# Causal attention with the keys on partitions: a first score pass for the maxima, no transposes of the probabilities, row sums on GpSimd

## The chip, the cores and the metric

The kernel runs on one core of one Trainium2 chip. The metric is the time of one execution on the device in microseconds. One core has five engines that take their instructions in order and meet through semaphores: TensorE (matmuls, PE in the profile; its weight loads are PEld), VectorE (DVE), ScalarE (ACT), GpSimd (POOL) and SyncE (SP), which only issues transfers here.

## The reference

One decoder layer over 2048 tokens of 1024 features, batch 1, in float32. Only the first sub-layer's attention changes; the rest is a convolution group beside it, a cross-attention into 256 memory tokens and an MLP of 4096 hidden features with a squared ReLU, each sub-layer between two RMS norms.

```python
def forgetting_attention(q, k, v, log_f):
    ...
    cum = jnp.cumsum(log_f, axis=1).transpose(0, 2, 1)
    ...
        logits = jnp.einsum("bqhd,bkhd->bhqk", qb, kb,
                            preferred_element_type=jnp.float32) * scale
        logits = logits + cum[:, :, q0:kl, None] - cum[:, :, None, :kl]
        ...
        mask = k_pos[None, :] <= q_pos[:, None]
        p = jax.nn.softmax(jnp.where(mask, logits, NEG_INF), axis=-1)
        outs.append(jnp.einsum("bhqk,bkhd->bqhd", p.astype(vb.dtype), vb))
```

There are 8 heads of 64 features. A softmax doesn't change with a number added to a whole row of logits, so the kernel adds only the bias of the key, not `cum` of the query.

## The kernel before

Activations are laid out with features on partitions and tokens along the free axis. The tokens go in four chunks of 512 (`TC`). Float32 products are made of float32r halves: `split` (a cast on ScalarE to the high part, a subtraction on VectorE for the low part) and `mm3`, three matmuls of high x high, high x low and low x high (L165 to L167).

The instructions are written by Python generators that are woven into one another by `drive`: a main stream (the input projections of a half, `mix_in`, then the MLP of chunks 0 to 3, `mlp`), beside it a side stream (`tail`: for each chunk the attention `attend`, then `mix_out` with the output projection, and `cross`), and the convolution's taps on VectorE as background. The numbers in `SCHED` set the ratios of the weave. The tile framework's scheduler then orders each engine's instructions by priorities and readiness, and puts in the semaphore waits. A tile of a tag takes one of the tag's slots (`BUFS`), in program order, and waits for the slot's earlier readers. `load` (L123) issues a transfer from GpSimd's queue, `store` (L126) one from SP's queue, which also brings the weights (L148).

`attend(c)` goes head by head through two blocks of 256 queries. `scores` puts queries on partitions: for each 128 queries and 512 keys two matmuls (L561, L562; the key tile holds high and low halves as 128 contraction rows, the query's high and its low part are repeated over both) into PSUM tag `sc`; VectorE adds the key bias (broadcast over the partitions by a transfer, tile `bias`) and keeps a running maximum, writing the row of logits `prow` to SBUF; the diagonal block's bias `dg` is masked by a GpSimd select (L544). When the row is whole, ScalarE makes the exponential in place and the row sum with it. `values` then turns each 128 x 128 block of `prow` with a TensorE transpose (L595) into PSUM tag `pt`, splits it into `pp`, and multiplies by the values (L611) into `o`. At the end of a head the two halves of `o` are added to `otmp`, which is stored to DRAM (`datt`); the row sums of the chunk go to DRAM (`drs`) and come back broadcast in `mix_out`.

Of the kernel before, what the change touches and what calls it, by code (L numbers as in the profile page):

```python
# [18 lines left out]
P = 128  # L19
# [3 lines left out]
TC = 512  # L23
# [27 lines left out]
# Chunk 0 takes also the slots that attention does not need then.  # L51
FIRST = dict(SIDE, rb="vk", y1="vk", q1="vk")
# [8 lines left out]
class Engine:  # L61
    """An engine; pinned, it takes its instructions in program order."""
# [18 lines left out]
class Trunk:  # L81
# [13 lines left out]
    # ---------------------------------------------------------------- tiles  # L95
# [64 lines left out]
    def mm3(self, ps, lhs, rhs, first=True, last=True):  # L160
        """ps (+)= sum over k of lhsT.T @ rhs, each operand a (high, low) pair."""
# [15 lines left out]
    def token_mean(self, ss, mean):  # L177
        """Mean over the features of ss ([128, w], partial sums): PSUM [128, w / 128], tokens on partitions."""
# [6 lines left out]
    def token_rstd(self, ss, mean):  # L185
        """1 / sqrt(mean + eps) per token, as token_mean."""
# [6 lines left out]
    def spread(self, r):  # L193
        """Values per token, [128, n] with tokens on partitions -> PSUM [128, n * 128], the same on every partition."""
# [12 lines left out]
    def pair8(self, w, name, tags):  # L207
        """Two high and two low [128, 4, w] tiles, in the order h l h l of the tags."""
# [3 lines left out]
    # ------------------------------------------------------------ constants  # L212
    def setup(self):
# [17 lines left out]
        self.carry = ct([NH, 1], "carry")  # L231
        self.rs = {c: ct([P, NH, 4], f"rs{c}") for c in range(NCH)}
# [5 lines left out]
        self.d_q = [[self.dram([2, 2, DH, TC], name="dq") for _ in range(NCH)] for _ in range(4)]  # L238
        self.d_v = [self.dram([NH, P, 8, P], name="dv") for _ in range(2)]
        self.d_nc = [self.dram([NH, HALF], name="dnc") for _ in range(2)]  # L240
# [6 lines left out]
    def setup_late(self):  # L247
# [6 lines left out]
        for t in range(4):  # L254
            self.store(self.d_u[t][:, :PAD], z)
        self.v.memset(self.wf.bitcast(F32), 0.0)
# [7 lines left out]
    # ---------------------------------------------------- memory keys/values  # L264
# [13 lines left out]
    def normed(self, xs, g, w, stag, out=None, tags=None):  # L278
        """rms_norm of xs, two [128, 4, w] tiles, in place; with tags also split, as in halves."""
# [20 lines left out]
    def halves(self, out, xs, w, tags):  # L300
        """out: the float32r (high, low) tiles of xs, two [128, 4, w] tiles."""
# [96 lines left out]
    def qk(self, h, t, ht, base):  # L398
        w = self.wtiles(self.i["w_in"][base + t], SIDE if t == 0 and base == 12 else MAIN)
        for j in range(2):  # L400
# [5 lines left out]
            for e in range(2):  # L406
                dst = (self.d_k[t][h][e, :, :, j * TC : (j + 1) * TC] if base == 12
                       else self.d_q[t][2 * h + j][e])
# [3 lines left out]
    def conv_push(self, c, t):  # L412
        """Background vector work: the depthwise convolution of channel tile t in chunk c, to DRAM."""
# [21 lines left out]
    def conv_norm(self, a, tag):  # L435
        """LayerNorm over the channels and swish of a ([128, 4, 512]), in place."""
# [22 lines left out]
    def gate(self, h, ht):  # L459
        """-cumsum(log_sigmoid(h @ w_f + b_forget)) of one half, to DRAM."""  # L460
# [29 lines left out]
        self.store(self.d_nc[h], u)  # L490

    # ------------------------------------------------------ forgetting attention
    def attend(self, c):
        """Queries of chunk c against all keys up to them, head by head."""
        nc = self.nc
        L = TC * (c + 1)
        small = L <= HALF
        pend = None
        for hd in range(NH):
            t, e = hd // 2, hd % 2  # L500
            if small:
                kv = self.tile("bk", [P, 2, L], F32R, name="kv")
# [582 lines left out]
```

## Time and profile before

| | us |
|---|---|
| median of 3 timed runs (lowest, highest) | 2849.29 (2844.85, 2852.8) |
| span of the profiled execution | 2843.6 |
| TensorE busy (share of the span) | 2779.2 (98%) |
| TensorE weight loads | 2310.6 (81%) |
| VectorE busy | 1967.2 (69%) |
| ScalarE busy | 1380.7 (49%) |
| GpSimd busy | 206.5 (7%) |

The profiled execution has no time of its own beside its span; the median of the runs is 5.7 us above it. Busy times of TensorE count pipelined matmuls, so a matmul's own duration is longer than the distance to the next one's start. The granted clock of TensorE is 0.996 of full speed in the mean.

### The profile page before, as it was taken

The numbers are of one execution on the slowest core, as the hardware profiler recorded it, in microseconds if no ns is written. First come the engines' busy times: TensorE is split into PE (matmuls) and PEld (weight loads), VectorE is DVE, ScalarE is ACT, GpSimd is POOL, SyncE is SP. The second block draws the span as 40 slices with busy tenths as digits, with TensorE's granted clock in tenths as the row PEclk, the third lists the DMA queues.
The fourth block names the chain that finished last, engine by engine and source line by source line (L and its number), as shares of the span: only waits on it lengthen the run. The fifth ranks groups of instructions, "written<-read, shape, count | busy, mean of one in ns | idle before, by whom it ended". The sixth has DMA issues, their size and how long they took to land.

```text
span 2843.6 us, 37412 instructions
## 1 busy us (share of the span) xinstructions
PE 2779.2 (98%) x14020; PEld 2310.6 (81%) x14020; DVE 1967.2 (69%) x3521; ACT 1380.7 (49%) x2164; POOL 206.5 (7%) x367
## 2 busy tenths in 40 slices
PE   7999999999999999999999999999999999999998
PEld 6889778888888887878888888788887888888887
DVE  7877896769787676788886645886665555743446
ACT  5323654345654445466554445665554445543332
POOL 0010300001110000012100001020100000000000
PEclk9999999999999999999999999999999999999999
DMA  5365744456544444455543435464524342343232
GB/s 168 117 217 170 174 128 163 141 164 200 154 137 132 124 136 145 149 151 175 138 142 119 146 108 166 129 197 129 155 94 128 126 145 93 130 144 97 96 97 81
DMA packets 141045, 398.32 MB, mean 140 GB/s; under 512 B 15248, under 2 KB 37904, under 8 KB 136000
## 3 DMA queue, kind: packets, MB, share of 16 engines
q1 hardware_dynamic: 99952, 262.40, 28.9%
q0 software_dynamic: 40912, 133.54, 16.4%
q8 instruction: 110, 1.80, 0.3%
q14 instruction: 71, 0.58, 0.1%
HBM read 330.68 MB, written 65.20 MB: 139 GB/s over the span
## 4 chain that ended last, share of the span: by engine, by line
PE 80%; issue 4%; DMA 4%; DVE 4%; ACT 2%; POOL 0%; SPq 0%; DVEq 0%; POOLq 0%; ACTq 0%
PE mm L165 18%; PE mm L166 18%; PE mm L167 18%; PE o L611 5%; PE sc L167 4%; PE sc L165 4%; PE sc L166 4%; PE pt L595 3%; PE sc L561 2%; PE sc L562 2%; DMA ks<-dk 1%; DVE acc L73 1%; DVE yacc L73 1%; DMA wr<-in_w_up_dram 1%; PE stat L182 1%
## 5 line engine op out<-in xcount | busy, mean ns | idle before, releaser
L73 ACT CAST wh<-wr 128x1024 fp32r<-128x1024 f32 x282 | 296.6, 1052 | 715.5 <-PE mm L166 634.1
L165 PE MATMUL mm<-h,wh 128*128 128x512 f32 x1504 | 597.6, 397 | 5.5 <-ACT h L73 2.6
L167 PE MATMUL mm<-h,wl 128*128 128x512 f32 x1504 | 596.9, 397 | 0.0
L166 PE MATMUL mm<-h,wh 128*128 128x512 f32 x1504 | 595.1, 396 | 1.7 <-DVE h L73 1.7
L73 DVE TENSOR_TENSOR wl<-wr,wh 128x1024 fp32r<-128x1024 f32 x282 | 345.5, 1225 | 277.2 <-ACT wh L73 276.0
L165 PE MATMUL mm<-hid,wh 128*128 128x512 f32 x992 | 395.3, 399 | 0.4 <-DVE yacc L73 0.4
L167 PE MATMUL mm<-hid,wl 128*128 128x512 f32 x992 | 392.8, 396 | 0.0
L166 PE MATMUL mm<-hid,wh 128*128 128x512 f32 x992 | 392.8, 396 | 0.0
L73 DVE SCALAR_TENSOR_TENSOR acc<-cu,convw,acc 128x512 f32<-128x512 f32 x480 | 356.9, 747 | 5.8
L165 PEld LDWEIGHTS mm<-h,wh 128*128 128x128 f32 x1504 | 283.9, 189 | 65.2 <-ACT h L73 2.9
L166 PEld LDWEIGHTS mm<-h,wh 128*128 128x128 f32 x1504 | 283.8, 189 | 60.1 <-DVE h L73 3.2
L167 PEld LDWEIGHTS mm<-h,wl 128*128 128x128 f32 x1504 | 283.6, 189 | 58.4
L73 DVE TENSOR_TENSOR yacc<-mm,yacc 128x512 f32<-128x512 f32 (+1 forms) x232 | 155.0, 669 | 160.3 <-PE mm L167 158.7
L73 DVE TENSOR_TENSOR pp<-pt,pp 128x512 fp32r<-128x512 f32 (+1 forms) x288 | 186.9, 656 | 68.0 <-ACT pp L73 66.6
L73 ACT CAST pp<-pt 128x512 fp32r<-128x512 f32 (+1 forms) x288 | 159.5, 560 | 124.6 <-PE pt L595 116.0
L165 PEld LDWEIGHTS mm<-hid,wh 128*128 128x128 f32 x992 | 186.3, 188 | 39.6 <-DVE yacc L73 1.5
L167 PEld LDWEIGHTS mm<-hid,wl 128*128 128x128 f32 x992 | 186.5, 188 | 38.5 <-issue 0.5
L166 PEld LDWEIGHTS mm<-hid,wh 128*128 128x128 f32 x992 | 186.6, 188 | 36.5 <-DVE hid L73 0.3
L595 PE MATMUL pt<-ident,prow 128*128 128x128 f32 x1088 | 199.3, 274 | 1.0 <-ACT prow L73 0.9
L73 ACT ACTIVATE prow<-prow,mx 128x128 f32<-128x128 f32 (+15 forms) x128 | 154.2, 1205 | 76.7 <-DVE mx L73 74.1
L73 DVE CUSTOM_DVE_ANT_0 prow<-sc,bias 128x512 f32<-128x512 f32 (+3 forms) x288 | 166.8, 596 | 34.3 <-PE sc L562 29.6
L611 PE MATMUL o<-pp,vv 128*128 128x256 f32 (+1 forms) x832 | 178.8, 299 | 8.6 <-DVE pp L73 7.9
(234 smaller groups left out, 4585.5 us busy)
## 6 DMA issues: line engine op xcount, KB each, us to landing
wr<-in_w_up_dram SPq DMA_DIRECT2D x128, 512.0 KB, 3.5
wr<-in_w_down_dram SPq DMA_DIRECT2D x128, 512.0 KB, 3.5
wr<-in_w_in_dram SPq DMA_DIRECT2D x32, 512.0 KB, 4.4
q<-dq POOLq DMA_DIRECT2D x64, 256.0 KB, 6.1
wr<-in_w_out_dram SPq DMA_DIRECT2D x32, 512.0 KB, 3.5
dx<-y SPq DMA_DIRECT2D x16, 1024.0 KB, 4.2
bias<-dnc POOLq DMA_DIRECT2D x32, 512.0 KB, 5.7
x<-in_x_dram POOLq DMA_DIRECT2D x12, 1024.0 KB, 5.9
```

Source lines behind the costliest of these rows:

```text
L73: ins = op(*args, **kw)
L165: mm(ps, ah, bh, start=first and j == 0, stop=False)
L166: mm(ps, ah, bl, start=False, stop=False)
L167: mm(ps, al, bh, start=False, stop=last and j == n - 1)
L182: self.nc.tensor.matmul(ps[:, t : t + 1], ss[:, t * P : (t + 1) * P], mean, start=True, stop=True)
L561: nc.tensor.matmul(ps[:, :w], q[:, 0, qs], ks[:, k0 : k0 + w], start=True, stop=False)
L562: nc.tensor.matmul(ps[:, :w], q[:, 1, qs], ks[:, k0 : k0 + w], start=False, stop=True)
L595: nc.tensor.transpose(pt[:, at : at + P], prow[t][:, (k0 + k) * P : (k0 + k + 1) * P], self.ident)
L611: nc.tensor.matmul(out, v[:, g + k], rhs, start=g == 0 and n == 0, stop=g == nk - 2 and n == 3)
```

## The change

Attention is done in two passes over a head, both generators; `peaks` runs some tiles ahead of `values` (n + 4 steps at the start of a chunk, n = 4(c + 1) key tiles, then one step of each in turn).

- `peaks` puts queries on partitions as before but computes one product only: the query's high part against the keys' high part, with two more contraction rows that hold the key bias's high and low part against ones (66 rows; L565). VectorE takes the maximum straight from PSUM; the diagonal block gets a mask first. The four negated maxima of a head, one column for each 128 queries, are transposed on TensorE (L587), copied to `mr`, stored to DRAM (`dm`) by SP's queue, and loaded by GpSimd's queue as one row of the query tile `q`.
- `values` puts keys on partitions: two matmuls (L608 with 128 rows, L609 with 67: the low query part, the bias rows and the row of negated maxima) give the shifted logits of 128 keys against up to 512 queries in PSUM tag `pt`. ScalarE makes the exponential from PSUM to the SBUF tile `p`; on the four diagonal tiles GpSimd zeroes the masked part (L614). `p` is split to `pp` and goes into the value product (L626) without a transpose. GpSimd adds `p` into an accumulator, the first tile's `p` (L621). At the end of the head four products with ones (L633) make the row sums.
- The gate also splits its bias and stores both parts (`d_kx`, in the place of `d_nc`); rows of ones are written to DRAM at the start. Tags: `vk` goes, `bq` and `ba` come, `vs` has 3 slots for 4; the y and rb tiles of chunk 0 are made of narrower ones.

```diff
-    "mk": 6, "bk": 7, "vk": 1,                            # 8 KB
+    "mk": 6, "bk": 7,
...
-    "ms": 4, "bs": 3, "vs": 4,                         # 2 KB
+    "ms": 4, "bs": 3, "bq": 2, "ba": 2, "vs": 3,
...
+        one = self.tile("mu", [NH, 2 * TC], name="one")
...
+        for t in range(4):
+            for c in range(NCH):
+                self.load(self.d_q[t][c][:, :, DH:].rearrange("e l o t -> (e l) o t"),
+                          one[:4].rearrange("p (o t) -> p o t", o=2))
...
-        self.store(self.d_nc[h], u)
+        self.split(e.bitcast(F32R), z.bitcast(F32R), u)
+        self.store(self.d_kx[h][:, 0], e)
+        self.store(self.d_kx[h][:, 1], z)
...
+        n = 4 * (c + 1)
...
+        p1, p2 = chain(peaks), chain(sums)
+        for _ in range(n + 4):
+            cost = next(p1, None)
+            if cost is not None:
+                yield cost
+        for cost in p2:
+            yield cost
+            cost = next(p1, None)
+            if cost is not None:
+                yield cost
...
+    def peaks(self, c, hd, T):
...
+        T["kb"] = kb = self.tile("bk", [P, L], F32R, name="kb")
+        for g, w, sl in self.halves_of(L):
+            self.load(kb[:DH, sl], self.d_k[t][g][e, 0, :, :w])
+            self.load(kb[DH : DH + 3, sl], self.d_kx[g][hd, :, :w])
+        q1 = self.tile("bq", [P, TC], F32R, name="q1")
+        self.load(q1[: DH + 2], self.d_q[t][c][e, 0])
+        mx = self.st([P, 4, 4], name="mx")
+        for t4 in range(4):
+            Lt = c * TC + (t4 + 1) * P
+            for n, k0 in enumerate(range(0, Lt, TC)):
...
+                nc.tensor.matmul(ps[:, :w], q1[: DH + 2, t4 * P : (t4 + 1) * P], kb[: DH + 2, k0 : k0 + w],
+                                 start=True, stop=True)
+                if k0 + w == Lt:
...
+                else:
+                    self.v.tensor_reduce(mx[:, t4, n : n + 1], ps, axis=AX.X, op=ALU.max)
+                yield 0.23 * w / TC
...
+        self.v.tensor_reduce(nm, mx[:, :, : c + 1], axis=AX.X, op=ALU.max, negate=True)
+        ps = self.ps("stat")
+        nc.tensor.transpose(ps[:4, :P], nm, self.ident)
+        mr = self.tile("row", [4, P], F32R, name="mr")
+        self.a.copy(mr, ps[:4, :P])
+        self.store(self.d_m[c][hd], mr.bitcast(F32))
+        self.load(T["q"][DH + 2 : DH + 3, 1], self.d_m[c][hd].rearrange("a b -> (a b)")[None])
...
-                        nc.tensor.transpose(
-                            pt[:, at : at + P], prow[t][:, (k0 + k) * P : (k0 + k + 1) * P], self.ident)
...
-                self.split(pp[:, 0, :at], pp[:, 1, :at], pt[:, :at])
...
+                nc.tensor.matmul(ps[:, q0:], ka[:, js], q[:, 0, q0:], start=True, stop=False)
+                nc.tensor.matmul(ps[:, q0:], kb[: DH + 3, js], q[: DH + 3, 1, q0:], start=False, stop=True)
+                p = self.tile("ba" if j == 0 else "bs", [P, TC], name="p")
+                self.a.activation(p[:, q0:], ps[:, q0:], AF.Exp)
+                if j >= 4 * c:
+                    dg = p[:, q0 : q0 + P]
+                    nc.gpsimd.affine_select(out=dg, in_=dg, pattern=[[1, P]], compare_op=ALU.is_ge, fill=0.0,
+                                            base=0, channel_multiplier=-1)
...
+                self.split(pp[:, 0, q0:], pp[:, 1, q0:], p[:, q0:])
+                if j == 0:
+                    acc = p
+                else:
+                    nc.gpsimd.tensor_tensor(out=acc[:, q0:], in0=acc[:, q0:], in1=p[:, q0:], op=ALU.add)
...
+                for l in range(2):
+                    nc.tensor.matmul(o[:, z:], v[:, k], pp[:, l, z:], start=k == 0 and l == 0,
+                                     stop=k == nk - 1 and l == 1)
...
+        for t in range(4):
+            nc.tensor.matmul(ps[:, t : t + 1], acc[:, t * P : (t + 1) * P], self.ones, start=True, stop=True)
+        self.a.copy(self.rs[c][:, hd], ps[:, :4])
```

Two places show how the order moves. On TensorE, in the attention of chunk 3, late in the chunk, the rows of before are these (`o<-pp,vv` is a value product, `pt<-ident,prow` a transpose, `sc<-ks,q` a score product, `mm<-h,wl` the main stream's):

```order
L595 MATMUL pt_17824<-ident,prow_17563 128x128
L167 MATMUL mm_17772<-h_2691_15806,wl_17769 128x512
L595 MATMUL pt_17824<-ident,prow_17564 128x128
L595 MATMUL pt_17824<-ident,prow_17563 128x128
L595 MATMUL pt_17824<-ident,prow_17564 128x128
L611 MATMUL o_17756<-pp_17817,vv_17330 128x256 [waits Activation_49]
L611 MATMUL o_17756<-pp_17817,vv_17330 128x256 [waits DVE_49]
L611 MATMUL o_17756<-pp_17817,vv_17330 128x256 x2
L561 MATMUL sc_17836<-ks_17729,q_17738 128x512
L562 MATMUL sc_17836<-ks_17729,q_17738 128x512
```

And in the order of the changed kernel, in head 6 of chunk 3 (`pt<-q,ka` and `pt<-q,kb` are the two score products of a key tile, `o<-pp,vv` the value products, `mm<-hid,wh` the main stream's):

```order
L609 MATMUL pt_17379<-q_16982,kb_16787 128x512
L608 MATMUL pt_17403<-q_16982,ka_16980 128x512 [waits Activation_49]
L626 MATMUL o_17279<-pp_17310,vv_16981 128x512 [waits Activation_49]
L609 MATMUL pt_17403<-q_16982,kb_16787 128x512
L165 MATMUL mm_17995<-hid_17316,wh_17977 128x512
L626 MATMUL o_17279<-pp_17310,vv_16981 128x512 [waits DVE_49]
L626 MATMUL o_17279<-pp_17370,vv_16981 128x512 [waits Activation_49]
L608 MATMUL pt_17417<-q_16982,ka_16980 128x512 [waits Activation_49]
L626 MATMUL o_17279<-pp_17370,vv_16981 128x512 [waits DVE_49]
L609 MATMUL pt_17417<-q_16982,kb_16787 128x512
L608 MATMUL pt_17431<-q_16982,ka_16980 128x512 [waits Activation_49]
L626 MATMUL o_17279<-pp_17384,vv_16981 128x512 [waits Activation_49]
```

The transposes are gone and scores and value products have 512 columns; a value product stands two to three key tiles behind its scores, each with a wait for ScalarE's cast or VectorE's subtraction, and in this part one row of twelve is the main stream's.

On GpSimd, around the end of a head of chunk 2, the rows of before are transfer issues (L123) with a select of the diagonal bias now and then:

```order
L123 DMA vv_12478<-dv_127 128x1024 [waits DMASW2_49,PE_49,Activation_49]
L123 DMA bias_12479<-dnc_130 128x512
L123 DMA vv_12478<-dv_128 128x512 [waits DMASW4_49]
L123 DMA bias_12814<-dnc_129 128x1024 [waits DMASW5_49,DVE_49,Pool_49]
L544 AFFINE_SELECT dg_12489<-bias_12479 128x256 [waits DMAHW4_49,DMASW3_49]
L123 DMA bias_12814<-dnc_130 128x512 [waits DMASW6_49]
L123 DMA q_12821<-dq_125 64x2x512 [waits DMASW7_49]
L123 DMA q_12821<-dq_125 64x2x512 [waits DMASW0_49]
```

In the changed kernel, around the end of head 2 of chunk 3 (p_15285 is that head's accumulator; `q<-dm` is the row of maxima of the head that comes next, and its wait on DMAHW0 is for the store by SP's queue; the `kb` tile belongs to the head after that):

```order
L614 AFFINE_SELECT p_15602<-p_15602 128x128 [waits DVE_49,Activation_49]
L621 TENSOR_TENSOR p_15285<-p_15285,p_15602 128x384 [waits Pool_49]
L123 DMA vv_15384<-dv_166 128x1024 [waits DMASW0_49,PE_49]
L123 DMA vv_15384<-dv_167 128x1024 [waits DMASW1_49]
L123 DMA q_15385<-dm_159 1x16x32 [waits DMAHW0_49,DMASW2_49]
L123 DMA kb_15588<-dk_110 64x1024 [waits DMASW3_49,PE_49]
L123 DMA kb_15588<-dkx_132 3x1024 [waits DMASW4_49]
L123 DMA kb_15588<-dk_111 64x1024 [waits DMASW5_49]
L123 DMA kb_15588<-dkx_133 3x1024 [waits DMASW6_49]
L614 AFFINE_SELECT p_15617<-p_15617 128x128 [waits DVE_49,Activation_49]
L614 AFFINE_SELECT p_15632<-p_15632 128x128 [waits Activation_49]
```

Selects and adds of the diagonal tiles now stand between the issues, and the last two selects of the head stand behind the load of the next head's maxima.

## Rows read from the trace of the kernel before

**Rows 1.** The page's first part: span, busy time, share and instructions by engine.

```profile
span 2843.6 us, 37412 instructions
...
PE 2779.2 (98%) x14020; PEld 2310.6 (81%) x14020; DVE 1967.2 (69%) x3521; ACT 1380.7 (49%) x2164; POOL 206.5 (7%) x367
```

**Rows 2.** Attention of chunks 0, 2, 3, all: us, then busy by engine, clock, DMA, GB/s.

```profile
282.00:372.00 90.00, 84.52 (x474) 68.21 (x474) 78.60 (x244) 55.99 (x127) 28.96 (x54) 1.00 0.70 179
...
1164.00:1440.00 276.00, 269.72 (x1460) 224.46 (x1459) 241.98 (x532) 158.68 (x248) 44.66 (x78) 0.98 0.52 155
1766.00:2096.00 330.00, 322.00 (x1811) 270.09 (x1810) 240.73 (x554) 192.84 (x289) 42.38 (x78) 1.00 0.50 149
sum 896.00, PE 872.53 PEld 732.51 DVE 726.59 ACT 525.50 POOL 147.71; mean PE 218.13 PEld 183.13 DVE 181.65 ACT 131.38 POOL 36.93
```

**Rows 3.** TensorE's timeline in three places: start, duration, line, operation, tiles, shape.

```profile
1901.09 0.39 PE L165 MATMUL mm<-h,wh 128*128 128x512 f32 x1
...
1902.22 0.39 PE L165 MATMUL mm<-h,wh 128*128 128x512 f32 x1
...
1904.18 0.60 PE L595 MATMUL pt<-ident,prow 128*128 128x128 f32 x4
1904.53 0.48 PE L165 MATMUL mm<-h,wh 128*128 128x512 f32 x1
...
2007.98 0.28 PE L611 MATMUL o<-pp,vv 128*128 128x256 f32 x1
2008.11 0.39 PE L166 MATMUL mm<-h,wh 128*128 128x512 f32 x1
```

**Rows 4.** Groups of TensorE's instructions by shape: count, busy us, mean ns, idle before.

```profile
L595 PE MATMUL pt<-ident,prow 128*128 128x128 f32 x1088 | 199.3, 274 | 1.0 <-ACT prow L73 0.9 <-DVE pp L73 0.2
L611 PE MATMUL o<-pp,vv 128*128 128x256 f32 x768 | 171.9, 303 | 8.2 <-DVE pp L73 7.4 <-ACT pp L73 0.6
...
L611 PE MATMUL o<-pp,kv 128*128 128x256 f32 x256 | 58.6, 301 | 1.8 <-DVE pp L73 0.6 <-ACT pp L73 0.5 <-DVE otmp L73 0.2
```

**Rows 5.** Groups by shape on VectorE and ScalarE: count, busy us, mean ns, idle before.

```profile
L73 DVE TENSOR_TENSOR pp<-pt,pp 128x512 fp32r<-128x512 f32 x224 | 152.4, 686 | 63.5 <-ACT pp L73 62.2
...
L73 DVE TENSOR_REDUCE mmx<-sc 128x2 f32<-128x512 f32 x32 | 21.9, 684 | 11.0 <-PE sc L167 10.9
...
L73 ACT CAST pp<-pt 128x512 fp32r<-128x512 f32 x224 | 130.1, 584 | 108.4 <-PE pt L595 100.0 <-DVE mx L73 3.1 <-DVE wl L73 2.6
```

**Rows 6.** Groups on GpSimd, then durations (min/median/max) of the selects of L544.

```profile
L544 POOL TENSOR_SCALAR_AFFINE_SELECT dg<-bias 128x256 f32<-128x256 f32 x64 | 36.0, 565 | 177.4 <-DMA datt<-otmp 77.9 <-DMA bias<-dnc 45.0 <-DVE mx L73 38.9
...
L123 POOL DMA_DIRECT2D bias<-dnc x48 | 26.6, 556 | 182.5 <-issue 88.0 <-PE sc L562 40.8 <-ACT h L73 22.8
...
masks.py:199 POOL TENSOR_SCALAR_AFFINE_SELECT ident<-ident 128x128 f32<-128x128 f32 x1 | 0.3, 318 | 0.1
...
L544 POOL TENSOR_SCALAR_AFFINE_SELECT dg<-bias x64: 398/426/1387, 282.4 to 2088.0; 128x256 f32<-128x256 f32 x64
```

**Rows 7.** Timeline of a select on GpSimd, a subtraction beside it, and the subtraction's group.

```profile
1878.56 0.45 POOL L544 TENSOR_SCALAR_AFFINE_SELECT dg<-bias 128x256 f32<-128x256 f32 x1
...
1878.59 0.97 DVE L73 TENSOR_TENSOR hid<-relu,hid 128x512 fp32r<-128x512 f32 x1
...
L73 DVE TENSOR_TENSOR hid<-relu,hid 128x512 fp32r<-128x512 f32 x128 | 88.4, 690 | 34.1 <-ACT hid L73 34.0
```

**Rows 8.** A copy's group; transfers (KB, us to landing); SP's waits (total, times, longest).

```profile
L73 ACT COPY rt<-stat 32x128 f32<-32x128 f32 x4 | 1.0, 256 | 0.8 <-PE stat L535 0.7
...
q<-dq POOLq DMA_DIRECT2D x64, 256.0 KB, 6.1
...
cu<-du POOLq DMA_DIRECT2D x16, 271.0 KB, 3.8
...
drs<-rt SPq DMA_DIRECT2D x4, 16.0 KB, 1.9
...
SPq L148 <- DVE wl L73: 1373.1, 262, 18.5
```

More of the change, by code (lines that the diff above doesn't have):

```diff
@@ L255, in setup_late @@
             self.store(self.d_u[t][:, :PAD], z)
+        one = self.tile("mu", [NH, 2 * TC], name="one")
+        self.v.memset(one, 1.0)
+        for h in range(2):
+            self.load(self.d_kx[h][:, 2], one[:, :HALF])
+        for t in range(4):
+            for c in range(NCH):
+                self.load(self.d_q[t][c][:, :, DH:].rearrange("e l o t -> (e l) o t"),
+                          one[:4].rearrange("p (o t) -> p o t", o=2))
         self.v.memset(self.wf.bitcast(F32), 0.0)
@@ L531, in attend, with chain @@
-        yield from self.values(*pend)
+            T = {}
+            peaks.append(self.peaks(c, hd, T))
+            sums.append(self.values(c, hd, T))
+        n = 4 * (c + 1)
+        def chain(gens):
+            for g in gens:
+                yield from g
+        p1, p2 = chain(peaks), chain(sums)
[8 more added lines that the diff above has]
+                yield cost
@@ L538, in attend, with halves_of @@
         self.store(self.d_rs[c].rearrange("a (b c) -> (a b) c", c=P), rt)
-    def scores(self, c, hd, b, ks, bias, q, small, rows):
-        nc = self.nc
-        L = c * TC + (b + 1) * QB
-        dg = self.tile("bs", [P, 2, P], name="dg")
-        nc.gpsimd.affine_select(
-            out=dg, in_=bias[:, L - QB : L].rearrange("p (t k) -> p t k", k=P), pattern=[[0, 2], [-1, P]],
-            compare_op=ALU.is_ge, fill=NEG, base=0, channel_multiplier=1)
-        if small:
-            pr = self.tile("bk", [P, 2, HALF], name="prow")
-            rows += [pr[:, 0, :L], pr[:, 1, :L]]
-        else:
-            rows += [self.tile("bk", [P, L], name="prow") for _ in range(2)]
-        mx = self.st([P, 2, 8], name="mx")
-        for t in range(2):
-            Lt = L - (1 - t) * P
-            p = rows[t][:, :Lt]
-            qs = slice(b * QB + t * P, b * QB + (t + 1) * P)
-            n = 0
-            for k0 in range(0, Lt, TC):
+    def halves_of(self, L):
+        for g in range((L + HALF - 1) // HALF):
+            w = min(HALF, L - g * HALF)
+            yield g, w, slice(g * HALF, g * HALF + w)
@@ L579, in scores @@
-                yield 0.43 * w / TC
-    def values(self, c, hd, b, prow, v):
+                        out=ps[:, :w], in0=ps[:, :w], in1=self.mask[:, TC - w :], op0=ALU.add, op1=ALU.max,
+                        scale=1.0, scalar=-3e38, accum_out=mx[:, t4, n : n + 1])
+                else:
+                    self.v.tensor_reduce(mx[:, t4, n : n + 1], ps, axis=AX.X, op=ALU.max)
+                yield 0.23 * w / TC
+            if t4 == 1:
+                T["ka"] = ka = self.tile("bk", [P, L], F32R, name="ka")
+                T["v"] = v = self.tile("bk", [P, L // P, P], F32R, name="vv")
+                T["q"] = q = self.tile("bu", [P, 2, TC], F32R, name="q")
+                for g, w, sl in self.halves_of(L):
+                    self.load(ka[:, sl], self.d_k[t][g][e, :, :, :w].rearrange("l d t -> (l d) t"))
+                    self.load(v[:, 8 * g : 8 * g + w // P], self.d_v[g][hd, :, : w // P])
+                for r in range(2):
+                    self.load(q[r * DH : (r + 1) * DH, 0], self.d_q[t][c][e, 0, :DH])
+                self.load(q[: DH + 2, 1], self.d_q[t][c][e, 1])
@@ L633, in residual, with pairs @@
         for k in range(KT):
-            y = ys[k // 4][:, k % 4]
+            y = ys[k // 2][:, k % 2]
             self.mul(y, y, r)
             self.add(y, y, xs[k // 4][:, k % 4])
-            if k % 4 == 3:
-                self.store(dst[:, k - 3 : k + 1], ys[k // 4])
+            if k % 2:
+                self.store(dst[:, k - 1 : k + 1], ys[k // 2])
             yield SCHED["y1"]
+    def pairs(self, g, role, name):
+        if role in g and role != "k":
+            return [self.tile(g[role], [P, 2, TC], name=name) for _ in range(2)]
+        y = self.tile(g["k"], [P, 4, TC], name=name)
+        return [y[:, 0:2], y[:, 2:4]]
     def mix_out(self, c, g):
@@ L655, in mix_out @@
             if b == 1:
-                self.mul(at, at, rb)
+                for k in range(2):
+                    self.mul(at[:, 2 * k : 2 * k + 2], at[:, 2 * k : 2 * k + 2], rb[k])
             self.split(hl[0][b], hl[1][b], (cu, at)[b])
@@ L684, in cross @@
         kt = self.ktiles(h2)
-        q2 = [self.tile(t, [P, 2, 2, TC], F32R, name="mq") for t in (g["k"], g.get("q1", g["k"]))]
+        q2 = []
         for f in range(MH):
+            if f == 2 and "q1" in g:
+                q2 += [[self.tile(t, [P, TC], F32R, name="mq") for t in g["q1"]] for _ in range(2)]
+            elif f % 2 == 0:
+                mq = self.tile(g["k"], [P, 2, 2, TC], F32R, name="mq")
+                q2 += [[mq[:, h, 0], mq[:, h, 1]] for h in range(2)]
             w = self.wtiles(i["w_mq"][f], g)
```

134 lines of the change are left out of this document (44 added, 90 removed).

## Prediction

> **What bounds the kernel now.** I read the page's busy times first: in a span of 2843.6 us TensorE is busy 2779.2 us, VectorE 1967.2, ScalarE 1380.7 and GpSimd 206.5 [rows 1]. So the kernel ends when TensorE has gone through its rows, and a change is worth the TensorE rows that it takes out, less the waits that it puts between them. The averages hide the stretches in which attention runs, so I then took a table by stretch, one stretch for the attention of each chunk [rows 2]. TensorE is busy 84.5 of 90 us in that of chunk 0, 269.7 of 276 in that of chunk 2, 322.0 of 330 in that of chunk 3 and 872.5 of 896 over the four: 23.5 us idle in all. VectorE is close behind: 87% of chunk 0's stretch and 88% of chunk 2's. GpSimd has most of its time free. Thus there are 23.5 us of waits to win in attention, and VectorE is the engine with the least room for being held up.
>
> A matmul's own duration overlaps the next one's, so rows are priced by the distance between starts [rows 3]: five matmuls of 512 columns take 1.13 us (0.227 each), one of 256 columns 0.13 (I use 0.12, nearer to half of 0.227), four transposes 0.35 (0.0875 each).
>
> **The change part by part.**
>
> TensorE, removed: 1088 transposes [rows 4] at 0.0875, 95 us. The two score passes keep their columns (2 x 512 per key tile and 512 queries in the place of 2 x 512 per 128 queries and 512 keys). The value products go from 1024 of 256 columns [rows 4] and 128 of 128 to fewer and wider ones, by the order 448 of 512 columns and 64 each of 384, 256 and 128, at prices by columns (0.227, 0.17, 0.12, 0.06) 124 us in the place of 131: 7 us less. Added: the peaks pass, 224 matmuls of 512 columns and 32 each of 384, 256 and 128, 51 + 11 = 62 us; 128 products of one column with ones for the row sums, no dearer than a transpose, 11 us; 32 small transposes, 3 us. Shorter moving operands can't go below these prices by much: the 128-column rows are 2 us in all. Sum: -95 - 7 + 62 + 11 + 3 = **-26 us**.
>
> TensorE's waits: the 23.5 us of the four stretches [rows 2] belong to chains that the change replaces (bias load, running maximum, exponential over a whole row). I take all of them out, **-24 us**, and put in the new ones below. At worst none goes.
>
> The chain of a key tile: the second pass does score, exponential, cast, subtraction, value product. Per full key tile of 512 queries TensorE has two score, two value and about one peaks matmul, 5 x 0.227 = 1.14 us. ScalarE has a cast (584 ns) and an exponential from PSUM (nearest row: the same cast, since it too reads 512 columns of PSUM): 1.17. VectorE has a subtraction (686) and a maximum over 512 columns (684): 1.37 [rows 5]. So where nothing of the main stream stands between, a tile costs 0.23 us more than its matmuls. The order shows where that is: heads 2 to 6 of chunk 0 and heads 5 to 7 of chunks 2 and 3, where the side stream runs with one main row to every three to eight of attention (first two fences of the order); that is 5 x 4 + 3 x 12 + 3 x 16 = 104 key tiles, 104 x 0.23 = **+24 us**. Elsewhere main matmuls, about as many as attention's, cover the difference; without that cover the other 216 tiles would cost 50 us more.
>
> GpSimd's adds: 288 of them replace sums that ScalarE gave with its exponential. No row of before is an add on GpSimd. The nearest is the select: 318 ns for 128 columns, 398 at the least and 565 in the mean for 256 [rows 6]. Continued at 80 ns per 128 columns that is 0.56 us for 512; twice the mean gives 1.13. The add reads two operands, so I take 1.13. A head of chunk 3 then has 13.5 full adds, 4 selects and 13 DMA issues of 0.56 [rows 6], 15.3 + 1.3 + 7.3 = 24 us, against 18 us of attention matmuls when dense and 40 of the stretch when not (330 / 8): alone it does not bound. The page "GPSIMD Engine Reference" of the Trainium skill, section 3.1, says that the Vector engine should keep elementwise work, an add taking GpSimd 1.96 times as long; on the 690 ns of a VectorE row here that would be an estimate of 1.35 us, which no run here shows yet.
>
> But adds also hold VectorE up. In before a subtraction of the MLP, both its operands in SBUF, started at 1878.59, 0.03 us behind a select of 0.45 us, and took 0.97 us, where its kind takes 0.69 in the mean [rows 7]: 0.28 us longer. The change makes all 320 subtractions of the value pass such (their source was PSUM), and puts an add beside each. At 0.28 us for each dense tile that is 104 x 0.28 = **+29 us**; at nothing, 0; at the full length of an add, 104 x 1.13 = 118 us. I take the row's figure, since the add, like the select, is over before many subtractions begin. "SBUF - State Buffer" in the Trainium skill, section "SBUF: two separate sides", speaks against the change here: a VectorE operation with two SBUF inputs and a GpSimd operation share a port pair under an exclusive lock, and the later waits out the earlier's whole length. The row agrees with that as far as a select of 0.45 us can tell; by the rule a longer add holds longer, toward the 118.
>
> The maximum's way back: for each head the four maxima go through a transpose (0.09), a copy (nearest row 256 ns), a store by SP (a 16 KB store lands in 1.9 us), a GpSimd load issue (0.56) and the landing, 3.8 us for the quickest of POOL's loads here and 6.1 for q [rows 8]: 6.6 to 8.9 us; with SP's 1.9 for the landing too, 4.7. The first L609 of the head needs it. Counted in the order from L587 to that row at the distances of [rows 3] there are 2.3 us in heads 3 to 6 of chunk 0, and 5.0 to 7.4 in most others. What is lacking over all heads sums to 10 us at 4.7, 32 at 6.6 and 89 at 8.9. SP's store also stands behind weight loads that wait 5.2 us each in the mean (1373.1 / 262), and GpSimd's load of the maxima, in waiting for that store, holds the selects of the head before that are queued behind it (last fence of the order). I take **+40 us**, a little over the middle value.
>
> Costed at nothing: the ones rows written to DRAM at the start (18 issues, 10 us of an otherwise idle GpSimd under the first projections; 10 us if they stood on the path); the gate's split and second store, under the half's projections; the narrower tiles of chunk 0.
>
> Sum: -26 - 24 + 24 + 29 + 40 = **+43 us**. The profiled execution's span of 2843.6 becomes 2887; the median of the runs, 2849.3, lies 5.7 above that span, so 2892 in the runs' terms.
>
> **The rivals.**
>
> *Faster:* the reordering hides it all. For: the program is a weave of streams and the order has two or more matmuls of the MLP or the projections beside most attention rows; before's own chain cost only 23.5 us of idle time. Against: the dense heads, and VectorE at 87 to 88%. If neither the 24 nor the 29 us appear and the way back costs 10: 2849 - 50 + 10 = 2809; if the waits of before stay too, 2833. Point 2821.
>
> *No change:* adds at 0.56 us that rarely meet a subtraction, so no 29, and the way back at the middle value: 2849 - 50 + 24 + 32 = 2855, down to 2845 with the way back at 22.
>
> *GpSimd becomes the bound:* an add that in its turn waits for VectorE's operations, and lies in front of the selects on which the diagonal's value products wait, and ahead of the row sums on TensorE (L633 waits for GpSimd's last add of a head, and TensorE takes its rows in order). With an add at 2.26 us, twice the price taken, a dense head of chunk 3 has 30.5 + 1.3 + 7.3 = 39 us of GpSimd for 18 of TensorE, of chunk 2 (9.5 adds) 30 for 14, of chunk 0 (1.5 adds, 9 issues) 10 for 4: 3 x 21 + 3 x 16 + 5 x 6 = 141 us in the place of the 24 + 29. That gives 2849 - 50 + 141 + 40 = 2980. It decides from some 1.5 us per add, waits included. For: the held-up subtraction [rows 7]. Against: GpSimd was at 13 to 32% of the stretches [rows 2].
>
> **How the numbers follow.** My forecast, some waits in the dense heads and at the maxima (2860 to 2930): 0.42. GpSimd as the bound (2930 to 3010): 0.23. No change (2840 to 2860): 0.12. Faster, 2800 to 2840: 0.23. The likeliest is the first, 2892. A measurement of this kernel can tell 0.3%, 8.5 us, from no change; of the no-change case two thirds lie within it and the rest falls to both sides: faster 0.25, same 0.08, slower 0.67. The range leaves out about a tenth at each end: 2817 to 2985. Within the likeliest case alone it is 2860 to 2930.
>
> **What would show it.** TensorE rows: no 128 x 128 transposes of prow, 224 one-matmul peaks, and the sum of distances 26 us down. Dense heads: in chunk 2 and 3 VectorE busy over 90% in heads 5 to 7, TensorE waiting before L626 for the subtraction; subtractions beside adds longer than 0.69 us, and adds over 1.1. Way back: TensorE idle before L609 on the DMA of dm, above all in heads 3 to 6 of chunk 0. GpSimd as bound would show as waits before L633, L614's readers and the p buffers' exponentials. I am wrong if adds come out near 0.56 us and subtractions stay at 0.69, or if the idle time before L609 is gone: then the time is below 2850.

## The result, and the profile after

The changed kernel takes 3064.61 us in the median (3061.45 to 3066.62, 4 runs); the kernel before took 2847.07 beside it. The ratio is 1.0766 (95% interval 1.075 to 1.0783): 217 us slower, where 43 were forecast.

The page of the changed kernel begins so, with the granted clock by slices (answers to [rows 1]); the last line is that of the kernel before:

```profile
span 3064.8 us, 35914 instructions
...
PE 2890.9 (94%) x13028; PEld 2315.0 (76%) x13028; DVE 2125.9 (69%) x3048; ACT 1395.2 (46%) x2293; POOL 680.4 (22%) x891
...
PEclk9999699998799999998899999999999999999999
...
PEclk9999999999999999999999999999999999999999
```

TensorE has fewer instructions than before and is yet busy 112 us longer, and idle 174 us (3064.8 - 2890.9) in the place of 64. Its granted clock was 9 tenths or more in each slice of before; now slices fall to 6, 7 and 8. The four attention stretches, from the first score row to the last value row of a chunk (answers to [rows 2]; the columns are those):

```profile
237.00:389.00 152.00, 140.89 (x765) 118.35 (x766) 111.51 (x207) 62.30 (x128) 63.55 (x120) 0.83 0.50 138
667.00:893.00 226.00, 196.71 (x972) 161.57 (x970) 181.83 (x288) 108.57 (x218) 116.24 (x154) 0.86 0.47 133
1251.00:1558.00 307.00, 266.30 (x1087) 197.92 (x1086) 268.75 (x386) 164.00 (x302) 188.62 (x215) 0.93 0.40 114
1886.00:2265.00 379.00, 335.81 (x1369) 247.03 (x1368) 304.58 (x412) 207.80 (x379) 225.07 (x243) 0.95 0.37 108
```

By the same marks they were 129, 191, 268 and 337 us before and are 152, 226, 307 and 379 now, 139 us more; and from the end of the last one the program takes 800 us to its end (706 before), since less of the main stream got done beside attention. GpSimd is busy in 42 to 61% of each (13 to 32% in [rows 2]), and the clock is 0.83 to 0.95. TensorE's longest waits: line, releaser, us in total, times, longest:

```profile
PE o L626 <- DVE pp L73: 67.4, 89, 3.0
PE stat L633 <- POOL p L621: 13.7, 13, 2.9
...
PE o L626 <- ACT pp L73: 10.9, 12, 3.2
...
PE pt L609 <- DMA q<-dm: 6.0, 4, 2.2
PE pt L608 <- ACT p L73: 5.2, 8, 1.4
```

The groups that answer to [rows 5] and [rows 6], and the products with ones:

```profile
L73 DVE TENSOR_TENSOR pp<-p,pp 128x512 fp32r<-128x512 f32 x224 | 249.1, 1129 | 45.6 <-ACT pp L73 44.7
...
L73 DVE TENSOR_REDUCE mx<-sc 128x1 f32<-128x512 f32 x192 | 129.4, 682 | 21.9 <-PE sc L565 21.2
...
L621 POOL TENSOR_TENSOR p<-p,p 128x512 f32<-128x512 f32 x192 | 291.2, 1517 | 107.3 <-ACT p L73 56.4 <-DVE pp L73 38.9 <-DVE mx L73 2.9
...
L614 POOL TENSOR_SCALAR_AFFINE_SELECT p<-p 128x128 f32<-128x128 f32 x128 | 60.7, 480 | 56.1 <-ACT p L73 52.3 <-DVE otmp L73 2.2 <-DVE pp L73 1.1
...
L633 PE MATMUL stat<-ones,p 128*128 128x1 f32 x256 | 45.5, 257 | 19.1 <-POOL p L621 13.7 <-ACT mr L73 4.2 <-DMA vv<-dv 0.5
```

A full subtraction takes 1129 ns, not 686. A full add takes 1517 ns in the mean. The maximum's way back (L609 waiting for q<-dm) is 6 us of TensorE's time. And L633 stands there 256 times, though the program issues 128: each float32 product is two rows.

What happens between an add and a subtraction is plain in the timeline. Two places, GpSimd first, then VectorE (start, duration):

```profile
2060.29 1.28 POOL L621 TENSOR_TENSOR p<-p,p 128x512 f32<-128x512 f32 x1 [3.62 <-ACT p L73]
...
2060.83 1.29 DVE L73 TENSOR_TENSOR pp<-p,pp 128x512 fp32r<-128x512 f32 x1 [1.33 <-ACT pp L73]
...
2205.04 1.27 POOL L621 TENSOR_TENSOR p<-p,p 128x512 f32<-128x512 f32 x1 [5.19 <-ACT p L73]
...
2205.98 0.88 DVE L73 TENSOR_TENSOR pp<-p,pp 128x512 fp32r<-128x512 f32 x1 [1.12 <-ACT pp L73]
```

The add of 2060.29 ends at 2061.57, and the subtraction that started 0.54 us into it ends at 2062.12, 0.55 later. The add of 2205.04 ends at 2206.31, and the subtraction that started 0.94 into it ends at 2206.86, again 0.55 later. Of the full adds that took under 1.30 us, 31 had a full subtraction start inside them; each of the 31 ended 0.55 or 0.56 us behind the add, wherever in the add it had started. So the subtraction waits until the add is over; it does not share a rate with it. Over all 224 full subtractions, the 61 that meet no add take 0.687 us in the mean, the 130 that start inside one 1.360, and the other 33, in which an add starts, 1.03.

TensorE's own rate in such a stretch, late in chunk 0 (two windows one behind the other, then rows of the second one's timeline):

```profile
300.00:324.00 24.00, 22.38 (x113) 17.27 (x111) 16.16 (x36) 10.09 (x27) 17.78 (x34) 1.00 0.52 139
324.00:376.00 52.00, 44.82 (x135) 32.86 (x136) 34.61 (x70) 20.92 (x53) 37.34 (x71) 0.52 0.41 106
...
340.29 0.58 PE L626 MATMUL o<-pp,vv 128*128 128x256 f32 x1 [0.52 <-DVE pp L73]
...
341.92 0.63 PE L609 MATMUL pt<-q,kb 67*128 67x512 f32 x1
342.35 0.63 PE L565 MATMUL sc<-kb,q 66*128 66x512 f32 x1
342.77 0.52 PE L609 MATMUL pt<-q,kb 67*128 67x384 f32 x1
...
346.25 0.59 PE L633 MATMUL stat<-ones,p 128*128 128x1 f32 x2 [0.73 <-ACT mr L73]
```

From 341.92 to 342.35 and to 342.77, matmuls of 512 columns stand 0.42 to 0.43 us apart, where [rows 3] had 0.227. In the first window the clock is 1.00 and TensorE busy in 22.4 of 24 us; in the second it is 0.52, the lower of its two levels (1.2 GHz of 2.4) nearly throughout, and that is the stretch in which it waits for subtractions and sums again and again (the idle times in brackets). Over the whole span the clock records have 227 us at the lower level, where there were 25 before.

### The profile page after: what moved, and what is told of

Same layout as the page of the kernel before. It is cut to its first block, busy times and chain, and to the rows that moved or that the text cites. A ratio compares the mean times of both kernels' runs of the same rounds, so it can differ in the third digit from the quotient of the medians.

```text
span 3064.8 us, 35914 instructions
## 1 busy us (share of the span) xinstructions
PE 2890.9 (94%) x13028; PEld 2315.0 (76%) x13028; DVE 2125.9 (69%) x3048; ACT 1395.2 (46%) x2293; POOL 680.4 (22%) x891
## 4 chain that ended last, share of the span: by engine, by line
PE 74%; DVE 12%; DMA 4%; POOL 4%; ACT 3%; issue 3%; POOLq 0%; ACTq 0%; DVEq 0%; SPq 0%
PE mm L166 18%; PE mm L165 18%; PE mm L167 17%; DVE pp L73 4%; PE sc L167 4%; PE sc L165 4%; PE sc L166 4%; POOL p L621 3%; PE o L626 2%; PE sc L565 1%; DVE acc L73 1%; DVE yacc L73 1%; DVE mx L73 1%; PE pt L609 1%; PE pt L608 1%
## 5 line engine op out<-in xcount | busy, mean ns | idle before, releaser
L621 POOL TENSOR_TENSOR p<-p,p 128x512 f32<-128x512 f32 (+3 forms) x288 | 370.8, 1288 | 111.3 <-ACT p L73 56.4
L73 DVE SCALAR_TENSOR_TENSOR acc<-cu,convw,acc 128x512 f32<-128x512 f32 x480 | 378.3, 788 | 7.2
L73 DVE TENSOR_TENSOR pp<-p,pp 128x512 fp32r<-128x512 f32 (+1 forms) x320 | 305.4, 969 | 84.3 <-ACT pp L73 83.1
L626 PE MATMUL o<-pp,vv 128*128 128x512 f32 (+3 forms) x640 | 244.9, 433 | 79.6 <-DVE pp L73 67.4
L626 PEld LDWEIGHTS o<-pp,vv 128*128 128x128 f32 x640 | 130.5, 215 | 161.6 <-DVE pp L73 121.9
L73 ACT CAST pp<-p 128x512 fp32r<-128x512 f32 (+1 forms) x320 | 174.8, 555 | 134.7 <-PE o L626 74.9
L73 ACT ACTIVATE p<-pt 128x512 f32<-128x512 f32 (+2 forms) x320 | 163.9, 531 | 150.7 <-PE pt L609 81.5
```

Of the source, the lines that this page charges most:

```text
L73: ins = op(*args, **kw)
L621: nc.gpsimd.tensor_tensor(out=acc[:, q0:], in0=acc[:, q0:], in1=p[:, q0:], op=ALU.add)
L626: nc.tensor.matmul(o[:, z:], v[:, k], pp[:, l, z:], start=k == 0 and l == 0, stop=k == nk - 1 and l == 1)
```

## The experiments

In all of them the scheduler orders anew, so an edit moves other rows too; only the two with the gap have the same order of TensorE's rows, row for row, as their parent. All ratios are to the kernel before, on the same chip in the same session. Between sessions the median of that kernel moved from 2844.9 to 2850.6 us, so a difference of times from two sessions is uncertain by some us. In the two runs without adds the row sums are those of a constant, so they are read for their time only.

| run | median us | ratio, 95% interval |
|---|---|---|
| changed kernel | 3064.6 | 1.0766 (1.075 to 1.0783) |
| no adds | 2927.5 | 1.0286 (1.0269 to 1.0303) |
| adds on VectorE | 2996.6 | 1.0528 (1.051 to 1.0546) |
| subtraction from PSUM | 3014.3 | 1.0593 (1.0577 to 1.0608) |
| no way back | 3047.7 | 1.0714 (1.0694 to 1.0734) |
| 128-byte gap in the kernel before | 2864.9 | 1.0062 (1.0042 to 1.0083) |
| the same gap in the changed kernel | 3045.9 | 1.0697 (1.0668 to 1.0727) |
| no first pass, adds on GpSimd | 3002.1 | 1.0549 (1.0526 to 1.0571) |
| no first pass, adds on VectorE | 2875.7 | 1.0099 (1.0076 to 1.0122) |
| ... and slots | 2815.8 | 0.9885 (0.9866 to 0.9904) |
| ... and more cover | 2770.5 | 0.9725 (0.9703 to 0.9747) |
| no adds, gap, more cover | 2873.6 | 1.0089 (1.0069 to 1.011) |
| gap, more cover | 2973.3 | 1.0445 (1.042 to 1.047) |

Theory A: an add on GpSimd holds up the subtraction, TensorE waits, and its clock falls after the waits. Theory B, the rival: the two passes are too dense and the maxima come late, whatever GpSimd does. Theory C: GpSimd is late because it is occupied, and the port pair of the prediction has no part in it.

**Without adds.**

```diff
-                else:
-                    nc.gpsimd.tensor_tensor(out=acc[:, q0:], in0=acc[:, q0:], in1=p[:, q0:], op=ALU.add)
```

> The 288 adds on GpSimd are left out; the products for the row sums read a constant, so the sums are those of ones. Theory A (an add holds the port that a subtraction of two SBUF operands needs, TensorE waits for the subtraction, and its clock falls after such waits): the 512-column subtractions go from 1129 ns back to 690, TensorE's wait for them from 67 us to under 20, granted clock from 0.963 to over 0.985, time 2840 to 2890. Theory B (the two-pass chain itself is too dense and the maxima come late, whatever GpSimd does): over 2980.

2927.5 us, so the adds cost 137 us of the 217. Subtractions are back at the length of [rows 5], and TensorE's wait for them fell from 67.4 us to 3.2:

```profile
span 2927.6 us, 35375 instructions
...
PE 2828.6 (97%) x13028; PEld 2289.7 (78%) x13028; DVE 1966.3 (67%) x3048; ACT 1388.0 (47%) x2293; POOL 307.9 (11%) x604
...
L73 DVE TENSOR_TENSOR pp<-p,pp 128x512 fp32r<-128x512 f32 x224 | 151.7, 687 | 62.5 <-ACT pp L73 61.4
...
PE o L626 <- DVE pp L73: 3.2, 7, 1.0
```

But 83 us stay over the kernel before, more than theory A allowed, and the granted clock came back to 0.979 only, not over 0.985: the adds are the larger part, not all. This run takes away the adds' collisions and their load on GpSimd together, so it speaks against theory B alone; A and C both fit it. Transfers queued behind the adds are not what it won: TensorE waits for the row of maxima (q<-dm) 6.3 us here and 6.0 in the changed kernel.

**Adds on VectorE.** `nc.gpsimd` becomes `self.v` in that line.

> The same 288 adds go to VectorE. Theory A: no collision is left, but VectorE gets 288 more operations, 240 full ones at 0.69 us, 165 us; subtractions at 0.69, time 2880 to 2960. Theory B: VectorE is the engine of the dense chain, so the time is no better than 3060. Theory C (GpSimd's occupancy, not the port, makes it late: row sums and selects stand behind adds): as A, but then the next run stays slow.

2996.6 us: 68 better than on GpSimd, although VectorE has 288 more operations now. It is above theory A's upper end, 2960, and under theory B's 3060; subtractions take 688 ns. It is 69 worse than without adds: the price of the adds as VectorE's work.

**The subtraction's source in PSUM.**

```diff
-                p = self.tile("ba" if j == 0 else "bs", [P, TC], name="p")
+                full = 0 < j < 4 * c
+                p = ps if full else self.tile("ba" if j == 0 else "bs", [P, TC], name="p")
...
-                    nc.gpsimd.tensor_tensor(out=acc[:, q0:], in0=acc[:, q0:], in1=p[:, q0:], op=ALU.add)
+                    nc.gpsimd.tensor_tensor(out=acc[:, q0:], in0=acc[:, q0:], in1=pp[:, 0].bitcast(F32) if full else p[:, q0:], op=ALU.add)
```

> All adds stay on GpSimd. For the key tiles off the diagonal and behind the first, the exponential is written back into PSUM, so the subtraction reads one operand from PSUM and one from SBUF; the add takes the high part of p, so the row sums leave out the low parts of those tiles. Theory A: subtractions of these tiles at 0.69 us beside adds of 1.27, time under 2930. Theory C: adds take as much of GpSimd as before, time over 3000.

Both kinds of subtraction stand side by side in this run, then its adds:

```profile
L73 DVE TENSOR_TENSOR pp<-pt,pp 128x512 fp32r<-128x512 f32 x168 | 114.8, 685 | 39.7 <-ACT pp L73 37.8
...
L73 DVE TENSOR_TENSOR pp<-p,pp 128x512 fp32r<-128x512 f32 x56 | 52.9, 945 | 21.6 <-ACT pp L73 20.6
...
L622 POOL TENSOR_TENSOR p<-p,pp 128x512 f32<-128x512 f32 x168 | 228.9, 1363 | 137.1 <-ACT pp L73 81.6 <-DVE pp L73 39.9 <-ACT wh L73 7.5
```

With one operand in PSUM the subtraction takes 685 ns beside adds of 1363; with both in SBUF 945. So the collision is one of SBUF operands, as theory A says of the mechanism. TensorE's wait for subtractions fell from 67.4 us to 21.0. But the time only fell by 50 us, to 3014, where theory A gave under 2930 and theory C over 3000. So theory C may hold for a part. GpSimd's selects on the diagonal tiles stand behind adds, and ScalarE's casts wait for the selects; in the changed kernel, in this run, and without adds:

```profile
ACT pp L73 <- POOL p L614: 44.1, 45, 6.4
...
ACT pp L73 <- POOL p L615: 54.6, 65, 2.3
...
ACT pp L73 <- POOL p L616: 18.4, 36, 2.7
```

Row sums that wait for the last add (L634, 18.2 us), adds that now wait for the cast, and the first and diagonal tiles, still in SBUF, may keep the rest. No run takes these apart: some 50 of the 137 us went with most of the collisions, and how the others divide between the collision and GpSimd's load stays open.

**No way back for the maxima.** The first pass runs, its result goes unused, and the row of q that held the maxima is the query's own gate bias, negated, stored once by the gate and loaded with q.

```diff
-        self.load(T["q"][DH + 2 : DH + 3, 1], self.d_m[c][hd].rearrange("a b -> (a b)")[None])
...
+                self.load(q[DH + 2 : DH + 3, 1],
+                          self.d_kx[c // 2][hd, 3:4, c % 2 * TC : (c % 2 + 1) * TC])
```

> The first pass runs in full, but its maxima are not used: each query's logits are shifted by its own gate bias instead (a row written once by the gate and loaded with q), so no head waits for the way back through DRAM. Theory A: 10 to 30 us better than the changed kernel, 3035 to 3055. Theory B: the way back and what GpSimd holds up in waiting for it are the larger part, under 2980.

3047.7 us, 17 better, inside theory A's 10 to 30. The way back is a small term.

**A gap of 128 bytes.** Every row of the main stream `mm<-h,wh` in the changed kernel was a little longer from start to start, even at the end of the program, where no attention runs: 0.2333 us ((2967.96 - 2961.66) / 27), against 0.227 in [rows 3].

```profile
2961.66 0.40 PE L165 MATMUL mm<-h,wh 128*128 128x512 f32 x1
...
2967.96 0.39 PE L165 MATMUL mm<-h,wh 128*128 128x512 f32 x1
```

The tile `vs` has slots of 2176 bytes per partition; with 3 of them instead of 4 everything behind moves, and the distance from the activations `h` to the weights, as the two programs lay out their tiles, changes from a multiple of 512 bytes (74240) to 92544, which is 384 over one. The edit is one unused tile behind the first `vs` tile:

```diff
+        gap = self.tile("gap", [P, 32], name="gap")
+        self.v.memset(gap, 0.0)
```

> The kernel before, with 128 unused bytes per partition between the main stream's activation tiles and all tiles behind them, so that the distance from its activations to its weights is no longer a multiple of 512 bytes, as in the changed kernel. Theory D (that distance slows the main stream's 512-column matmuls from 0.227 to 0.232 us from start to start): the rows mm<-h at 0.231 to 0.233, 4512 of them at 0.005 more, 20 to 28 us slower, 2865 to 2875. Against it (the distances are longer because of what the other engines read and write): 2840 to 2852.

> The changed kernel with the same 128 bytes, which here bring the distance back to a multiple of 512. Theory D: mm<-h back at 0.227, 15 to 28 us faster than the changed kernel, 3035 to 3050. Against it: 3058 to 3070.

In the kernel before it costs 0.62% (0.42 to 0.83), some 18 us, a little under theory D's 20 to 28; in the changed kernel it saves 19 (3064.6 to 3045.9). Both bear out theory D. In the profile of the former, activations that moved with the weights (hid) and those that did not (h) follow one another:

```profile
2713.02 0.39 PE L167 MATMUL mm<-hid,wl 128*128 128x512 f32 x1
...
2720.50 0.39 PE L167 MATMUL mm<-hid,wl 128*128 128x512 f32 x1
2720.72 0.40 PE L165 MATMUL mm<-h,wh 128*128 128x512 f32 x1
...
2722.35 0.39 PE L166 MATMUL mm<-h,wh 128*128 128x512 f32 x1
```

hid: 33 steps in 7.48 us, 0.2267. h: 7 steps in 1.63 us, 0.233. So 19 us of the change are due to where a tile landed. This holds for the main stream's rows: the score rows sc<-ks,q of the kernel before, whose tiles lie a multiple of 512 bytes apart too, stand 0.231 apart in the median, with the gap and without it, so the distance is not the whole rule.

**No first pass.** With the gate bias as the shift the exponent of a query and an earlier key is their scaled product plus a sum of log gates. That sum is never above zero, so softmax needs no maximum as long as the scaled products alone stay small, and `peaks` is left with its loads, issued one head ahead. The gap is in.

> No first pass: the logits of a query are shifted by its own gate bias (as in the run without the way back), the loads of a head are issued one head ahead, and the 128 bytes are in. GpSimd still adds. Takes out 62 us of peaks rows on TensorE and 150 to 215 us of maxima on VectorE. Theory A: the adds go on holding up the subtractions, so most of their 137 us stay: 2900 to 2980. Theory B (the first pass and VectorE's load make the chain too dense): under 2850.

> As the run before, with the adds on VectorE, which has had the maxima taken off it. Theory A: no add stands beside a subtraction, VectorE's load is under that of the kernel before, TensorE's rows 90 us shorter than the kernel before's: 2760 to 2840, faster than both kernels. Theory B: the same, since the first pass is gone; if the chain of score, exponential, cast, subtraction, product is itself too long for the order, it stays over 2850.

With the adds on GpSimd 3002.1 us, above what either theory gave, on VectorE 2875.7. The same 288 adds are 126 us dearer on GpSimd, now that VectorE has time. That alone fits theory C too; the waits of the run with the adds on GpSimd speak for A as the larger part (argued from waits, not taken apart), since TensorE waits four times as long for subtractions as for the sums that need the last add, and subtractions take 1200 ns:

```profile
L73 DVE TENSOR_TENSOR pp<-p,pp 128x512 fp32r<-128x512 f32 x224 | 264.0, 1200 | 123.5 <-ACT pp L73 122.7
...
PE o L596 <- DVE pp L73: 73.6, 95, 2.8
...
PE stat L603 <- POOL p L591: 18.1, 22, 3.7
```

But 2875.7 missed the 2840 that A allowed; over 2850 was forecast for a chain that is itself too long. The waits with the adds on VectorE show where it waits (ScalarE, then TensorE):

```profile
ACT p L73 <- DMA datt<-otmp: 52.0, 17, 6.0
...
PE pt L578 <- ACT p L73: 30.4, 18, 4.8
PE o L596 <- ACT pp L73: 29.1, 15, 5.0
```

An exponential of a head's fourth to sixth key tile waits 3 us each, 17 times, until the last head's otmp has landed in DRAM, because p and otmp share three slots.

**Slots, then cover.**

```diff
-    "ms": 4, "bs": 3, "bq": 2, "ba": 2, "vs": 3,
+    "ms": 4, "bs": 4, "bq": 2, "ba": 2, "vs": 3,
...
-                ps = self.ps("pt")
+                ps = self.ps("sc" if j % 2 else "pt")
...
-        tmp = self.tile("bs", [P, TC], name="otmp")
+        tmp = self.tile("bq", [P, TC], name="otmp")
```

> The run without the first pass and with adds on VectorE, and three slot changes: a head's otmp has slots of its own (it held one of the three slots of p until its store had landed; ScalarE waited 52 us for that), p has 4 slots, the scores alternate between the PSUM tags pt and sc. If slots make its waits (30 us before L578, 29 before L596): 2810 to 2850, equal to or better than the kernel before. If the chain itself is too dense where the side stream runs alone: no better than 2865.

2815.8 us, 60 better, and under the kernel before; the three slot changes were not tried one by one. Then the declared cost, by which the weave deals out the main stream:

```diff
-                yield 0.9 * (TC - q0) / TC
+                yield 1.2 * (TC - q0) / TC
```

> As the run before, with the declared cost of a key tile raised from 0.9 to 1.2, so that the weave puts more of the main stream beside each tile and attention takes longer. If density is what is left: 2790 to 2840, better than the run before by 10 to 40 us. If not, the same within 10 us, or worse where the side stream no longer fits beside the main one.

2770.5 us, another 45 better and 2.75% (2.53 to 2.97) under the kernel before. Its page and longest waits:

```profile
span 2773.4 us, 34353 instructions
...
PE 2698.5 (97%) x12676; PEld 2220.3 (80%) x12676; DVE 1934.6 (70%) x2857; ACT 1379.7 (50%) x2264; POOL 306.9 (11%) x569
...
PE stat L182 <- DVE nss L73: 12.2, 1, 12.2
PE stat L198 <- DVE rstd L73: 8.2, 6, 5.4
PE pt L574 <- DMA ka<-dk: 5.8, 1, 5.8
```

> The changed kernel without its adds (the row sums read a constant, as in the first run), with the 128 bytes and with declared costs raised by a third in both passes. Theory B in its smaller form (what is left without adds, 83 us over the kernel before, less 19 for the 128 bytes, is the dense chain): 2850 to 2890. If the weave has no part in it: 2900 to 2912.

> The changed kernel, adds on GpSimd and first pass included, with the 128 bytes and the declared costs raised by a third. Without adds that weave gave 2874 in the place of an estimated 2909. If the adds' harm (some 137 us) is a matter of too little main work beside the chain, it shrinks here: 2930 to 2990. If the held-up subtractions cost the same whatever stands beside them, the weave saves only the 35 us that it saved without adds: 3005 to 3020.

Without adds the same weave gives 2873.6, 35 us under the 2909 that the first run and the gap would make; with them 2973.3, 73 us under the 3045.9 with the gap alone. So cover hides some of the adds' harm (2930 to 2990 was forecast for that), and at this cover the adds still cost 100 us.

## Why the prediction was wrong

The sign and the place were right: slower, through waits in the second pass. The size was five times too small, and the range did not hold it.

- **TensorE's rows, -26.** The transposes are gone, as forecast. The row sums were priced at 128 rows and are 256: some 11 us more at the same price. And the rows that the change does not touch grew longer by the placement, 19 us by the gap run: this was in no term.
- **The waits of before, -24.** Idle time of TensorE is 174 us, not 64 less 24. Whether the old waits went can't be told from the new ones.
- **GpSimd's adds beside VectorE, +29.** This is the step that failed: "I take the row's figure, since the add, like the select, is over before many subtractions begin". The figure was 0.28 us, from a subtraction that met a select of 0.45 us. An add takes 1.27 us at least, and the program makes the two meet: both start from the same exponential, the add at once, the subtraction after a cast of 620 ns, in the middle of the add. The row of [rows 7] held the law already: its select ended at 1879.01 and its subtraction at 1879.56, 0.55 behind, as all 31 above; what carries over is not the 0.28 but the rest of the add. 130 of 224 full subtractions began inside an add and were on the mean 0.67 us late; all 224 lost 98 us of VectorE's time (224 x (1.129 - 0.69)). I also let only 104 dense tiles pay. The adds as a whole measured 137 us, of which some 50 went with most of the collisions in the PSUM run. The upper bound in the text, 118, was nearer, and so was the rule that was set beside it ("SBUF - State Buffer" of the Trainium skill, section "SBUF: two separate sides"): the later operation waits out the earlier one's whole length; the 31 collisions agree with it to 0.01 us. For the add's length, the estimate of 1.35 us from "GPSIMD Engine Reference" of the Trainium skill, section 3.1, stands against 1.27 to 1.29 us for the undisturbed ones here.
- **TensorE's clock.** It had no term at all. The mean granted clock is 0.963 where it was 0.996; with two levels, 1.2 and 2.4 GHz, that is some 227 us of the span at the lower one (2 x 0.037 x 3064.8) in the place of 23. TensorE was busy in 194 us of that time, 14 before, and a row of 512 columns takes 0.42 to 0.43 us there for 0.23; by an estimate from these figures the slow rows cost some 80 us, beside the 110 us more of idle time. No run holds the clock while it keeps the waits, so this split is not tested. Over the runs the clock is higher where TensorE is idle less: 0.979 at 99 us of idle time without adds, 0.982 at 83 with more cover too, 0.985 at 75 in the fastest. It does not go step by step: the run with the subtraction's source in PSUM has 0.965 at 135 us.
- **The dense chain, +24.** Right in kind as far as the runs show: with adds and placement taken out (137 + 19) 61 us are left, and a different weave alone wins 35 of them. What the other 26 are, no run says.
- **The way back, +40.** 17 us measured, with the quicker landing nearer the truth. L609 waited 6 us in all.
- **The rivals.** "GpSimd becomes the bound" gave 2980 and named the waits before L633 (13.7 us on TensorE) and the selects; it was nearer than the forecast, and yet 85 us short. With GpSimd busy in 42 to 61% of the stretches, TensorE's longest wait is the one for subtractions (67.4 us), not the one for GpSimd's sums. But its selects do hold the chain up: ScalarE's casts wait 44.1 us for them, 18.4 without adds, so the rival has a part in it; how much time, no run says.

## What to carry to other kernels

Where an elementwise operation on an idle GpSimd and a subtraction on VectorE with both operands in SBUF start from one event, price the subtraction as ending 0.55 us behind GpSimd's operation. A faster place for the adds was VectorE itself, by 68 us with the maxima there and by 126 without. In the dense stretches here the clock was lower where TensorE waited, so such a wait can cost more than its length; count the main rows between a chain's links before calling it hidden. Compare also the rows that an edit does not touch: here 19 us came from a tile's new address.

## What the runs showed of the hardware that was not expected

- The main stream's 512-column matmuls stand 0.2267 us from start to start where their moving tile and weights lie a multiple of 512 bytes apart, and 0.233 with 128 or 384 bytes over that. The two gap runs have their parents' order of rows on every engine, with one memset more. Other distances were not tried, the attention's rows do not follow it, and why it is so stays open.
- A subtraction with two SBUF operands that meets an add on GpSimd ends 0.55 us behind the add's end, whenever it began (31 of 31 undisturbed adds in the changed kernel), while it takes 0.687 alone.
- A one-column float32 product (L633) is two rows of TensorE, each with its own weight load.
